# A 256-token hybrid layer on one core: the products of a weight piece in two runs instead of in turn

## The chip, the core and the metric

The kernel runs on one core of one Trainium2 chip. The time is the device time of one execution in microseconds (us). Times of single instructions come from one execution that the hardware profiler recorded. TensorE is called PE in the rows, VectorE DVE, ScalarE ACT, GpSimd POOL, SyncE SP. The start of a matmul is a recorded time; its end is modelled, so that neighbouring matmuls overlap in the rows. What a matmul costs in a stream is therefore read from one start to the next, and not from its duration.

## What is computed

One layer of a bidirectional encoder on 256 tokens of 2048 features, in float32:

```
x = x + 1/2 SwiGLU_1(RMSNorm(x))                  2048 -> 5632 -> 2048
h = RMSNorm(x);  [q|k|v|u|y] = h @ W_in
A = attention(q, k, v);  R = (scan_fwd(conv u) + scan_bwd(conv u)) * gelu(y)
x = x + concat([A, R]) @ W_out
x = x + 1/2 SwiGLU_2(RMSNorm(x))
x = x + sigmoid(RMSNorm(x) @ W_gate) * (p @ W_ple)
out = RMSNorm(x)
```

## The kernel before

**Two parts of 12 bits.** To come near float32 with matmuls that keep fewer bits, every operand is held as a sum of a high and a low part (`split`, line 80: ACT casts the high part, line 81, and DVE subtracts it from the source, line 82). A product of two operands is then high by high, high by low and low by high. The activations lie as `[P, 2, S]`: for 128 features the 256 high parts and beside them the 256 low parts.

**The pair.** `unit_mm` (line 108) makes the three products with two matmuls. The wide one (line 115) has the weights' high part `wh` as stationary operand and streams all 512 columns of the activations into a bank `ps` of PSUM. The small one (line 111) has the weights' low part `wl` as stationary operand and streams the 256 high columns into the second half of the same bank. Each matmul brings its own weight load.

**The unit.** `unit` (line 130) makes 128 output features for all tokens. It walks over the contraction in steps of 128 features, one pair each, all of them added up in one bank. The weights come as one tile per DMA (`weights`, line 119), 16 steps wide (or 11 for `w2`), and are split in pieces of eight steps (8 and 8, or 8 and 3); `spl_pair` gives a piece its two buffers, `whi` and `wlo`, of which there are four each. The FFNs' first layers, the projections to u and y, the output projection and the gate use units of 16 steps. The FFNs' second layers (`w2`, 32 units in each FFN) use units of 22 steps in four pieces (8, 3, 8, 3).

**Other users of PE.** `lead` (line 235) does the first three units together while the first operands arrive. `proj` (line 146) makes q, k and v the other way round: there the activations are stationary and 512 columns of split weights are streamed, three matmuls for each product (`mm3`, lines 89 to 91). The gates of the scans (`scan_job`) use `mm3` with 256 columns. `embed` uses two pairs per call. At the end the last two gate units take their small products in one run (line 633) and their wide ones in halves of 256 columns (line 642).

**Order.** A scheduler lays out each engine's list in advance, from the order in which the code is written, from priorities and from its own simulated times. PE works its list off in order. A piece's first wide matmul waits for ACT's cast, its first small one for DVE's subtraction, and the two buffers come free when PE has done with them.

Of the kernel before, what the change touches and what calls it, by code (L numbers as in the profile page):

```python
# [18 lines left out]
P = 128  # L19
D = 2048  # L20
S = 256
NH = S // P
FF = 5632
C = 512
NKD = D // P
# [3 lines left out]
EPS = 1e-6  # L29
HD = 128  # L30
GRID_W = 64
THETA = 10000.0

# Columns of the packed per-channel parameters.
O_G1, O_GM, O_G2, O_GP, O_GF = 0, 16, 32, 48, 64
# [5 lines left out]
LEAD = (0, 0), (1, 0), (0, 1)  # L41
# [4 lines left out]
def hymba_layer(ctx, tc, xT, pT, w1a, w3a, w2a, win, wqkv, lruw, wout, w1b, w3b, w2b,  # L46
# [31 lines left out]

# [1 line left out]
    def split(src, hi, lo, eng=None):  # L80
# [25 lines left out]

# [1 line left out]
    def unit_mm(ps, wh, wl, a, first, last, cols=slice(0, S)):  # L108
        """a: [P, 2, S], the parts of the activations; the small terms go to the second half."""
        def small():  # L110
            nc.tensor.matmul(ps[:, 1, cols], lhsT=wl, rhs=a[:, 0, cols], start=False, stop=False)  # L111

        if last and not first:
            small()
        nc.tensor.matmul(ps[:, :, cols], lhsT=wh, rhs=a[:, :, cols], start=first, stop=last and not first)  # L115
        if first or not last:
            small()

# [11 lines left out]
    def unit(aT, srcs, nk):  # L130
        """aT: [P, 2, S] per 128 features of the contraction; srcs: DRAM tiles of nk of them."""
        ps = acc.tile([P, 2, S], F32, tag="acc", name="acc")
        at, n = 0, nk * len(srcs)
        for src in srcs:
            for wh, wl in weights(src, nk):
                unit_mm(ps, wh, wl, aT[at], at == 0, at == n - 1)
                at += 1
        tick()
        return ps
# [4 lines left out]

# [1 line left out]
    def proj(aT, srcs):  # L146
# [27 lines left out]

# [1 line left out]
    warm = sml.tile([P, 1], F32, tag="warm", name="warm", bufs=1)  # L176
# [17 lines left out]
    def rsqrt(dst, ssum, n, width):  # L194
        """dst = (ssum / n + EPS) ** -0.5"""
        v = sml.tile([P, 8], F32, tag="rs_v", name="rs_v")[:, :width]
        nc.vector.tensor_scalar(v, ssum, 1.0 / n, EPS, op0=ALU.mult, op1=ALU.add)
        nc.gpsimd.tensor_tensor(dst, v, mhalf[:, :width], op=ALU.pow)

    def inv_rms(*ssq, halves=range(NH), keep=True):  # L200
        """ssq: [P, S], squares summed over blocks of features; all their partitions add up.
        -> 1 / rms per token, as [P tokens, NH] and as [P, S] on every partition."""
        ps = trp.tile([P, 2, S], F32, tag="tr", name="sums")
        n = len(halves)
        for i, h in enumerate(halves):
            for j, s in enumerate(ssq):
                nc.tensor.matmul(ps[:, 0, i:i + 1], lhsT=s[:, h * P:(h + 1) * P], rhs=ones[:, 0:1],
                                 start=j == 0, stop=j == len(ssq) - 1)
        r = sml.tile([P, NH], F32, tag="inv", name="inv", bufs=2)[:, :n]
        rsqrt(r, ps[:, 0, :n], D, n)  # L210
        dg = tmp("dg")
        pb = trp.tile([P, 2, S], F32, tag="tr", name="rows")
        for i in range(n):
            cols = slice(i * P, (i + 1) * P)
            nc.vector.tensor_scalar(dg[:, cols], ident, r[:, i:i + 1], None, op0=ALU.mult)
            nc.tensor.matmul(pb[:, 0, cols], lhsT=ones, rhs=dg[:, cols], start=True, stop=True)
        if not keep:
            return r, pb[:, 0, :n * P]
        rB = sml.tile([P, S], F32, tag="rB", name="rB", bufs=2)
        nc.scalar.copy(rB, pb[:, 0, :])  # L220
        return r, rB

    def add_square(ssq, n, cols=slice(0, S), eng=None):
        """ssq (+)= xs[n] ** 2"""
        if n == 0:
# [9 lines left out]
    def lead():  # L235
        """The first operands in small pieces, in the order of their use; two units at once."""
        aT = act_tiles()
        ps = [acc.tile([P, 2, S], F32, tag="acc", name="acc") for _ in LEAD]
        at = 0
        for n in PIECES:  # L240
# [10 lines left out]
            for m in range(len(LEAD)):  # L251
                split(raw[m][:, js, :], sp[m][0][:, js, :], sp[m][1][:, js, :])
                if m == 0:
                    for k in range(at, at + n):
                        split_gain(xs[:, k, :], par_at(O_G1 + k), aT[k][:, 0, :], aT[k][:, 1, :])
            for k in range(at, at + n):
                for m in range(len(LEAD)):
                    unit_mm(ps[m], sp[m][0][:, k % 8, :], sp[m][1][:, k % 8, :], aT[k], k == 0, k == NKD - 1)
            at += n
# [46 lines left out]

# [1 line left out]
    begun = [None]  # L308
    early = tc.cur_priority + 1000
    am, (rm, rmB) = ffn(*lead(), w1a, w3a, w2a, O_GM)  # L310

# [1 line left out]
    late = tc.cur_priority  # L313
# [11 lines left out]

    # -8 softplus(-lambda), with log1p(e) = 2 atanh(e / (2 + e))
    cneg = const.tile([P, 16], F32, name="cneg")
# [21 lines left out]

# [1 line left out]
    def conv(o, i, blk):  # L351
# [6 lines left out]

# [1 line left out]
    def scan_job(g, u):  # L360
# [65 lines left out]

# [1 line left out]
    def head_rms(src, nh, half):  # L428
        """src: [P tokens, nh HD] -> 1 / rms of each head."""
        ss = sml.tile([P, 4], F32, tag="qss", name="qss")[:, :nh]  # L430
# [7 lines left out]
    def rotate(src, nh, half, m):  # L438
        """[P tokens, nh HD] times the norm's gain, rotated."""
        sv = src.rearrange("p (h d) -> p h d", d=HD)  # L440
# [24 lines left out]
    def transposed(blocks, at, evac):  # L465
        """blocks[h]: [P tokens, .]; two blocks of columns from at on."""
        ps = trp.tile([P, 2, S], F32, tag="tr", name="tr")
# [75 lines left out]

# [1 line left out]
    def y_job(g, y):  # L545
# [24 lines left out]

# [1 line left out]
    ap, (_, rpB) = ffn(a2, inv_rms(ssq2), {}, w1b, w3b, w2b, O_GP)  # L572

# [1 line left out]
    pr = mtile("pr")  # L575
# [9 lines left out]
    def embed(n):  # L585
# [3 lines left out]
        ps = trp.tile([P, 2, S], F32, tag="tr", name="pe")  # L589
        for k in range(2):  # L590
            unit_mm(ps, wh[:, k, :], wl[:, k, :], pp[:, k, :, :], k == 0, k == 1)
        t = tok.tile([P, S], F32, tag="tok", name="pe")
# [22 lines left out]

    # The last features go one half of the tokens after the other; so does the last norm.
    pe = [embed(n) for n in (NKD - 2, NKD - 1)]
# [42 lines left out]
def _units(w, kc=None):  # L660
    """[K, N] -> [N / P, K / (kc P), P, kc P], each tile contiguous."""
    k, n = w.shape
# [5 lines left out]
def _tiles(w):  # L668
    """[K, N] -> [N / C, K / (4 P), P, 4 C], each tile contiguous."""
    k, n = w.shape  # L670
# [4 lines left out]
def _cols(v):  # L675
    """[..., n P] -> [P, ... n]: a channel per partition."""
    return np.ascontiguousarray(v.reshape(-1, P).T)


def _features(v):  # L680
    """[S, n P] -> [P, n S]"""
    return np.ascontiguousarray(v.T.reshape(-1, P, S).transpose(1, 0, 2)).reshape(P, -1)
# [64 lines left out]
```

## Time and profile before

| | |
|---|---|
| median of 3 runs | 1936.04 us (1935.06 to 1936.06) |
| span of the profiled execution, first to last instruction | 1934.1 us |
| PE busy | 98% of the span |
| DVE, ACT, POOL busy | 64%, 51%, 15% |
| share of PE in the chain that ended last | 94% |
| mean granted clock of PE | 0.992 |

The span and the median differ by 1.9 us, which lie outside the first and the last instruction. Shares of busy time are averages over the span; the chain that ended last goes back from the last instruction to what released it, and so on to the start. Nearly all of that chain is matmuls of the two lines 115 and 111, one behind the other.

### The profile page before, as it was taken

Reading aid. Unit: us, or ns where it says so; the run is one execution under the profiler, and the core shown is the slowest. Engines: PE = TensorE matmul, PEld = TensorE weight load, DVE = VectorE, ACT = ScalarE, POOL = GpSimd, SP = SyncE. Lnnn points to the kernel's source line nnn. Section 1 sums busy time; section 2 is a strip of 40 time slices with the busy share of each in tenths; the row PEclk is TensorE's granted clock in tenths of the full one; section 3 lists DMA queues with packets and bytes.
Section 4 is the critical chain, followed back from the end, with each engine's and each line's share of the span. In section 5 each row is a group of like instructions: output and inputs, shape, how many; then the busy total and the mean of one; then the engine's idle time right before and its main releaser. Section 6 shows DMA issues by size and latency. Waiting matters only on the chain.

```text
span 1934.1 us, 26888 instructions
## 1 busy us (share of the span) xinstructions
PE 1895.7 (98%) x10664; PEld 1639.5 (85%) x10664; DVE 1231.6 (64%) x1723; ACT 980.7 (51%) x1490; POOL 286.4 (15%) x231
## 2 busy tenths in 40 slices
PE   7999999999999999998999999999999999999997
PEld 5888888888888888876888888888888888888886
DVE  6766655566666556888777656665556666665686
ACT  4544444444444455586664545454344445545553
POOL 3111100001111000374211111110001111001132
PEclk8999999999999999999999999999999999999998
DMA  6555545565555456534445555554565555555642
GB/s 219 189 193 182 188 163 180 188 211 195 177 193 182 160 192 207 195 137 150 150 152 193 178 188 182 192 174 166 192 213 182 189 186 185 209 188 182 210 161 79
DMA packets 61262, 350.74 MB, mean 181 GB/s; under 512 B 6480, under 2 KB 12112, under 8 KB 31056
## 3 DMA queue, kind: packets, MB, share of 16 engines
q1 hardware_dynamic: 61136, 349.03, 52.9%
q8 instruction: 83, 1.36, 0.3%
q14 instruction: 43, 0.35, 0.1%
HBM read 346.90 MB, written 2.10 MB: 180 GB/s over the span
## 4 chain that ended last, share of the span: by engine, by line
PE 94%; DVE 2%; ACT 2%; DMA 1%; issue 1%; SPq 0%; POOL 0%; POOLq 0%; DVEq 0%; ACTq 0%
PE acc L115 60%; PE acc L111 30%; DVE gate L410 1%; DMA raw<-in_w3a 0%; DVE wlo L82 0%; PE acc L642 0%; PE pe L115 0%; DMA lead<-in_w1a 0%; SPq L101 0%; PE po L508 0%; PE tr L481 0%; PE acc L90 0%; PE acc L91 0%; ACT whi L81 0%; PE acc L89 0%
## 5 line engine op out<-in xcount | busy, mean ns | idle before, releaser
L115 PE MATMUL acc<-aT,whi 128*128 128x512 f32 x3296 | 1156.3, 400 | 10.0 <-DVE aT L86 10.0
L82 DVE TENSOR_TENSOR wlo<-raw,whi 128x1024 fp32r<-128x1024 f32 x722 | 799.9, 1116 | 301.6 <-ACT whi L81 294.9
L81 ACT CAST whi<-raw 128x1024 fp32r<-128x1024 f32 x722 | 689.9, 956 | 482.8 <-PE acc L115 422.0
L111 PE MATMUL acc<-aT,wlo 128*128 128x256 f32 x3296 | 894.6, 282 | 0.0
L115 PEld LDWEIGHTS acc<-aT,whi 128*128 128x128 f32 x3296 | 608.1, 189 | 145.7 <-DVE aT L86 13.1
L111 PEld LDWEIGHTS acc<-aT,wlo 128*128 128x128 f32 x3296 | 624.0, 189 | 20.6
L115 PE MATMUL acc<-hT,whi 128*128 128x512 f32 x1408 | 493.2, 399 | 0.0
L111 PE MATMUL acc<-hT,wlo 128*128 128x256 f32 x1408 | 385.1, 281 | 0.0
L115 PEld LDWEIGHTS acc<-hT,whi 128*128 128x128 f32 x1408 | 260.5, 188 | 59.6
L290 POOL TENSOR_TENSOR s<-s,rB 128x256 f32<-128x256 f32 x88 | 110.5, 1255 | 1103.7 <-ACT s L287 1103.7
L111 PEld LDWEIGHTS acc<-hT,wlo 128*128 128x128 f32 x1408 | 265.8, 189 | 6.4
L301 DVE SCALAR_TENSOR_TENSOR xs<-acc,xs 128x256 f32<-128x256 f32 x128 | 53.8, 420 | 142.7 <-PE acc L115 142.7
L142 ACT COPY z<-acc 128x256 f32<-128x256 f32 x88 | 32.7, 372 | 156.3 <-PE acc L115 156.3
L142 ACT COPY u<-acc 128x256 f32<-128x256 f32 x88 | 32.7, 371 | 154.4 <-PE acc L115 154.4
L230 POOL TENSOR_TENSOR ssq<-ssq,sqr 128x256 f32<-128x256 f32 x58 | 54.2, 934 | 339.8 <-ACT sqr L229 339.8
L115 PE MATMUL acc<-mixT,whi 128*128 128x512 f32 x256 | 89.5, 399 | 1.4 <-DVE mixT L82 1.4
L143 DVE TENSOR_TENSOR u<-acc,u 128x256 f32<-128x256 f32 x88 | 37.2, 423 | 83.2 <-ACT u L142 83.1
L143 DVE TENSOR_TENSOR z<-acc,z 128x256 f32<-128x256 f32 x88 | 37.3, 424 | 83.0 <-ACT z L142 83.0
L111 PE MATMUL acc<-mixT,wlo 128*128 128x256 f32 x256 | 69.3, 281 | 0.0
L115 PEld LDWEIGHTS acc<-mixT,whi 128*128 128x128 f32 x256 | 47.1, 188 | 12.0 <-DVE mixT L82 1.8
L85 ACT ACTIVATE aT<-xs,par_sb 128x256 fp32r<-128x256 f32 x64 | 31.5, 507 | 47.9 <-DVE xs L301 43.9
L86 DVE SCALAR_TENSOR_TENSOR aT<-xs,par_sb,aT 128x256 fp32r<-128x256 f32 x64 | 48.0, 762 | 6.9 <-ACT aT L85 3.4
(169 smaller groups left out, 1051.4 us busy)
## 6 DMA issues: line engine op xcount, KB each, us to landing
raw<-in_w2a SPq DMA_DIRECT2D x64, 704.0 KB, 4.0
raw<-in_w1b SPq DMA_DIRECT2D x44, 1024.0 KB, 5.0
raw<-in_w3b SPq DMA_DIRECT2D x44, 1024.0 KB, 4.9
raw<-in_w2b SPq DMA_DIRECT2D x64, 704.0 KB, 4.0
raw<-in_w3a SPq DMA_DIRECT2D x43, 1024.0 KB, 4.9
raw<-in_w1a SPq DMA_DIRECT2D x42, 1024.0 KB, 4.9
raw<-in_win SPq DMA_DIRECT2D x16, 1024.0 KB, 4.9
raw<-in_wout SPq DMA_DIRECT2D x16, 1024.0 KB, 4.8
```

The costliest lines, as they stand in the source:

```text
L81: nc.scalar.copy(hi, src)
L82: (eng or nc.vector).tensor_tensor(lo, src, f32(hi), op=ALU.subtract)
L85: nc.scalar.activation(hi, src, AF.Copy, scale=gain)
L86: nc.vector.scalar_tensor_tensor(lo, src, gain, f32(hi), op0=ALU.mult, op1=ALU.subtract)
L111: nc.tensor.matmul(ps[:, 1, cols], lhsT=wl, rhs=a[:, 0, cols], start=False, stop=False)
L115: nc.tensor.matmul(ps[:, :, cols], lhsT=wh, rhs=a[:, :, cols], start=first, stop=last and not first)
L142: nc.scalar.copy(t, ps[:, 1, cols])
L143: nc.vector.tensor_tensor(t, ps[:, 0, cols], t, op=ALU.add)
L230: (eng or nc.gpsimd).tensor_tensor(ssq[:, cols], ssq[:, cols], t, op=ALU.add)
L290: nc.gpsimd.tensor_tensor(s, s, rB, op=ALU.mult)
L301: nc.vector.scalar_tensor_tensor(xs[:, n, :], ps[:, j, :], 0.5, xs[:, n, :], op0=ALU.mult, op1=ALU.add)
L410: nc.vector.tensor_tensor_scan(i[d][:, k, rev], a[d][:, k, rev], r[d][:, k, rev], 0.0, op0=ALU.mult, op1=ALU.add)
```

## The change

`unit_mm` is gone. `unit_mms` takes the weights of a whole piece and issues all its wide matmuls first and then all its small ones. The number of matmuls, their operands and shapes, the DMAs and the splits are the same. A bank is now opened by the piece's first wide matmul and closed by its last small one. `unit`, `lead` and `embed` call it with pieces of 8 (or 3), of 1 to 4, and of 2 steps.

```diff
-    def unit_mm(ps, wh, wl, a, first, last, cols=slice(0, S)):
-        """a: [P, 2, S], the parts of the activations; the small terms go to the second half."""
-        def small():
-            nc.tensor.matmul(ps[:, 1, cols], lhsT=wl, rhs=a[:, 0, cols], start=False, stop=False)
-
-        if last and not first:
-            small()
-        nc.tensor.matmul(ps[:, :, cols], lhsT=wh, rhs=a[:, :, cols], start=first, stop=last and not first)
-        if first or not last:
-            small()
+    def unit_mms(ps, ws, acts, first, last):
+        n = len(ws)
+        for i in range(n):
+            nc.tensor.matmul(ps, lhsT=ws[i][0], rhs=acts[i], start=first and i == 0, stop=False)
+        for i in range(n):
+            nc.tensor.matmul(ps[:, 1, :], lhsT=ws[i][1], rhs=acts[i][:, 0, :], start=False,
+                             stop=last and i == n - 1)
...
         for src in srcs:
-            for wh, wl in weights(src, nk):
-                unit_mm(ps, wh, wl, aT[at], at == 0, at == n - 1)
-                at += 1
+            ws = weights(src, nk)
+            for j in range(0, nk, 8):
+                part = ws[j:j + 8]
+                unit_mms(ps, part, aT[at:at + len(part)], at == 0, at + len(part) == n)
+                at += len(part)
...
-            for k in range(at, at + n):
-                for m in range(len(LEAD)):
-                    unit_mm(ps[m], sp[m][0][:, k % 8, :], sp[m][1][:, k % 8, :], aT[k], k == 0, k == NKD - 1)
+            for m in range(len(LEAD)):
+                unit_mms(ps[m], [(sp[m][0][:, k % 8, :], sp[m][1][:, k % 8, :]) for k in range(at, at + n)],
+                         aT[at:at + n], at == 0, at + n == NKD)
...
-        for k in range(2):
-            unit_mm(ps, wh[:, k, :], wl[:, k, :], pp[:, k, :, :], k == 0, k == 1)
+        unit_mms(ps, [(wh[:, k, :], wl[:, k, :]) for k in range(2)], [pp[:, k, :, :] for k in range(2)],
+                 True, True)
```

In the lists below `whi` marks a wide matmul (line 115 before, line 113 in the changed kernel) and `wlo` a small one (line 111 before, line 115 in the changed kernel). A number behind a name is that of the buffer; each `aT` buffer holds four steps of the contraction and each `hT` buffer two.

PE's list before, in the first layer of FFN 1, from the end of one unit (bank `acc_1826`) to the start of the next (`acc_1869`):

```order
L111 MATMUL acc_1826<-aT_110,wlo_1834 128x256
L115 MATMUL acc_1826<-aT_110,whi_1833 128x512
L111 MATMUL acc_1826<-aT_110,wlo_1834 128x256 x2
L115 MATMUL acc_1826<-aT_110,whi_1833 128x512
L115 MATMUL acc_1869<-aT_107,whi_1872 128x512
L111 MATMUL acc_1869<-aT_107,wlo_1873 128x256
```

The same unit in the changed kernel:

```order
L113 MATMUL acc_1826<-aT_107,whi_1829 128x512 x4
L113 MATMUL acc_1826<-aT_108,whi_1829 128x512 x4
L115 MATMUL acc_1826<-aT_107,wlo_1830 128x256 x4
L115 MATMUL acc_1826<-aT_108,wlo_1830 128x256 x4
L113 MATMUL acc_1826<-aT_109,whi_1833 128x512 x4
L113 MATMUL acc_1826<-aT_110,whi_1833 128x512 x4
L115 MATMUL acc_1826<-aT_109,wlo_1834 128x256 x4
L115 MATMUL acc_1826<-aT_110,wlo_1834 128x256 x4
L113 MATMUL acc_1869<-aT_107,whi_1872 128x512 x4
```

Where the two kinds took turns, with two in a row only at the unit's end, eight wide ones now stand in a row and then eight small ones.

PE's list in the changed kernel at the start of the second layer of FFN 1, the first half of a unit of 22 steps:

```order
L113 MATMUL acc_2420<-hT_360,whi_2423 128x512 x2
L113 MATMUL acc_2420<-hT_361,whi_2423 128x512 x2
L113 MATMUL acc_2420<-hT_362,whi_2423 128x512 x2
L113 MATMUL acc_2420<-hT_363,whi_2423 128x512 x2
L115 MATMUL acc_2420<-hT_360,wlo_2424 128x256 x2
L115 MATMUL acc_2420<-hT_361,wlo_2424 128x256 x2
L115 MATMUL acc_2420<-hT_362,wlo_2424 128x256 x2
L115 MATMUL acc_2420<-hT_363,wlo_2424 128x256 x2
L113 MATMUL acc_2420<-hT_364,whi_2427 128x512 x2
L113 MATMUL acc_2420<-hT_365,whi_2427 128x512
L115 MATMUL acc_2420<-hT_364,wlo_2428 128x256 x2
L115 MATMUL acc_2420<-hT_365,wlo_2428 128x256
```

Here runs of eight and runs of three follow each other.

PE's list in the changed kernel at the start of the mixing stage, where the last step's activations (the fourth step of `aT_5684`) come latest (`sums` adds up the squares for the norm):

```order
L113 MATMUL acc_6896<-aT_5683,whi_6903 128x512 x4
L113 MATMUL acc_6896<-aT_5684,whi_6903 128x512 x3
L113 MATMUL acc_6947<-aT_5681,whi_6950 128x512 x4
L113 MATMUL acc_6947<-aT_5682,whi_6950 128x512 x4
L115 MATMUL acc_6947<-aT_5681,wlo_6951 128x256 x4
L115 MATMUL acc_6947<-aT_5682,wlo_6951 128x256 x4
L113 MATMUL acc_6947<-aT_5683,whi_6954 128x512 x4
L208 MATMUL sums_6836<-ones_103,ssq_5685 128x1 x2
L113 MATMUL acc_6896<-aT_5684,whi_6903 128x512
L115 MATMUL acc_6896<-aT_5683,wlo_6904 128x256 x4
L115 MATMUL acc_6896<-aT_5684,wlo_6904 128x256 x4
```

The scheduler has put twenty matmuls of the second unit (`acc_6947`) between the first unit's 15th and its 16th wide one.

## Rows read from the trace of the kernel before

**Rows 1.** The page: busy time per engine, granted clock in 40 slices, chain by engine

```profile
PE 1895.7 (98%) x10664; PEld 1639.5 (85%) x10664; DVE 1231.6 (64%) x1723; ACT 980.7 (51%) x1490; POOL 286.4 (15%) x231
...
PEclk8999999999999999999999999999999999999998
...
PE 94%; DVE 2%; ACT 2%; DMA 1%; issue 1%; SPq 0%; POOL 0%; POOLq 0%; DVEq 0%; ACTq 0%
```

**Rows 2.** Groups: line, engine, operation, out<-in, shape, count | busy, mean ns | idle before

```profile
L115 PE MATMUL acc<-aT,whi 128*128 128x512 f32 x3296 | 1156.3, 400 | 10.0 <-DVE aT L86 10.0
...
L115 PE MATMUL acc<-hT,whi 128*128 128x512 f32 x1408 | 493.2, 399 | 0.0
...
L115 PE MATMUL acc<-mixT,whi 128*128 128x512 f32 x256 | 89.5, 399 | 1.4 <-DVE mixT L82 1.4
```

**Rows 3.** Timeline of PE at a unit's end: start, length (modelled), line, operation, count

```profile
600.22 0.40 PE L111 MATMUL acc<-aT,wlo 128*128 128x256 f32 x2
600.46 0.63 PE L115 MATMUL acc<-aT,whi 128*128 128x512 f32 x2
600.93 0.28 PE L111 MATMUL acc<-aT,wlo 128*128 128x256 f32 x1
601.05 0.40 PE L115 MATMUL acc<-aT,whi 128*128 128x512 f32 x1
```

**Rows 4.** Chain that ended last, in time: start, time in the chain, what

```profile
334.92 0.47 PE acc L115 x2
342.69 0.47 PE acc L115 x2
...
549.75 0.47 PE acc L115 x2
...
594.97 0.47 PE acc L115 x2
```

**Rows 5.** Timeline of PE in the mixing stage: scan gates (tr) and a projection

```profile
824.63 0.28 PE L89 MATMUL tr<-uc_hi,gw_hi 128*128 128x256 f32 x1
...
824.98 0.28 PE L89 MATMUL tr<-uc_hi,gw_hi 128*128 128x256 f32 x1
...
825.58 0.28 PE L91 MATMUL tr<-uc_hi,gw_lo 128*128 128x256 f32 x1
...
826.06 0.40 PE L89 MATMUL acc<-whi,aT 128*128 128x512 f32 x1
826.30 0.40 PE L90 MATMUL acc<-wlo,aT 128*128 128x512 f32 x1
826.53 0.39 PE L91 MATMUL acc<-whi,aT 128*128 128x512 f32 x1
826.76 0.40 PE L89 MATMUL acc<-whi,aT 128*128 128x512 f32 x1
...
827.23 0.39 PE L91 MATMUL acc<-whi,aT 128*128 128x512 f32 x1
...
827.90 0.39 PE L91 MATMUL acc<-whi,aT 128*128 128x512 f32 x1
...
831.53 0.28 PE L89 MATMUL tr<-uc_hi,gw_hi 128*128 128x256 f32 x1
```

**Rows 6.** Timeline of PE near the end: 24 small matmuls of line 633 in a row

```profile
1907.08 3.04 PE L633 MATMUL small<-aT,wlo 128*128 128x256 f32 x24
1909.96 0.52 PE L642 MATMUL acc<-aT,whi 128*128 128x256 f32 x3
```

**Rows 7.** Waits of PE: engine, line, waited for, us in total, times, longest

```profile
PE acc L90 <- DVE wlo L82: 11.3, 4, 4.7
PE acc L115 <- DVE aT L86: 10.0, 8, 3.2
```

**Rows 8.** Busy time by stretch, the mixing stage's middle, with the clock behind POOL

```profile
830.00:912.00 82.00, 69.47 (x313) 56.37 (x312) 66.05 (x61) 58.29 (x94) 51.00 (x22) 0.94 0.41 141
```

**Rows 9.** Groups: ACT's casts of weight pieces, with the idle time before them

```profile
L81 ACT CAST whi<-raw 128x1024 fp32r<-128x1024 f32 x722 | 689.9, 956 | 482.8 <-PE acc L115 422.0 <-PE acc L91 17.2 <-issue 15.6
```

## The prediction

> **What bounds the kernel now.** First the page [rows 1]: PE is busy 98% of the span, holds 94% of the chain that ended last, and its granted clock stands at nine tenths or more in 38 of 40 slices. PE's list is the path; DVE (64%) and ACT (51%) are beside it nearly everywhere. So the question is not who waits, but how closely PE can start one matmul after another, and whether that depends on their order.
>
> Second, the groups [rows 2]: 3296 + 1408 + 256 wide matmuls are 206 x 16, 64 x 22 and 16 x 16 steps. From the code, the 206 hold the lead's three units, so 219 units of 16 steps are outside it; each has two pieces of eight, 438. The 64 units of `w2` have two pieces of eight and two of three. Together that is **566 pieces of eight and 128 pieces of three**; what else uses pairs (the lead's 48, the embedding's 32) is a sixtieth of the whole.
>
> Third, the price of a piece now. In the chain [rows 4] the pair of wide matmuls that closes one unit and opens the next stands at 549.75 and again, eight units later, at 594.97: 45.22 us for 16 pieces of eight, **2.826 us a piece**, 0.3533 a pair. For `w2` it stands at 334.92 and 342.69: 7.77 us for 22 pairs, again 0.353, so a piece of three costs 1.060. At full clock these streams have no gaps: what a pair costs is PE's own pace.
>
> Fourth, what runs cost. Outside the lead the trace has no run of more than two wide matmuls from `unit_mm`, but the mixing stage has the changed kernel's pattern with other operands [rows 5]: 12 small ones of a scan's gates (256 columns) and then a long run of 512-column ones of a projection, each with a weight load of its own.
> - Small ones after wide ones: from 824.63 to 826.06 twelve in 1.43 us; the first eight, up to 825.58, in **0.95 us**. The first three take 0.35 us (to 824.98).
> - Wide ones after small ones: the first eight, from 826.06 to 827.90, in **1.84 us**. They don't start at their final pace: the first three take 0.70 us (to 826.76), while from 827.23 to 831.53 there are 19 in 4.30 us, 0.2263 each. The switch costs some 0.03 us, spread over the first five.
> - Small ones of exactly this kind in a long run [rows 6]: 24 in 2.88 us, 0.120 each, the gates' pace.
>
> So a pair costs 0.353 us in alternation, and 0.2263 + 0.120 = 0.346 us if its halves stand in long runs. Alternation pays for a switch at every pair.
>
> **The change part by part.**
> *A piece of eight* becomes one run of eight wide and one of eight small: 1.84 + 0.95 = 2.79 us instead of 2.826, a gain of 0.036. One row stands for 2.79 and is rounded to a hundredth, so 0.036 is good to about 0.01. 566 x 0.036 = **20.4 us**, and 15 to 26 with the rounding.
> *A piece of three*: 0.70 + 0.35 = 1.05 instead of 1.060; 128 x 0.010 = **1.3 us** (0 to 2.5).
> *Unit ends*: the old order put two small and two wide side by side there; this is inside the 2.826. In the new order a unit begins and ends as any piece does.
> *Buffers and waits*: nothing is added. A piece's first wide one follows the piece before it as it did, so ACT's cast is due when it was; the first small one comes 1.84 us later in its piece, where it came one wide matmul (0.235) later, so DVE's part is due later. The `whi` buffer comes free one run of small ones earlier (0.95 us); ACT, which is idle 422 us waiting for PE to free such buffers [rows 9], casts that much earlier into a queue that PE reaches in the same order. Taken at nothing; this hides behind the three other buffers, and without them a late cast would delay a whole run.
> *Stage starts*: the last step's activations are now due in the middle of the second piece, after 2.79 + 7 x 0.23 = 4.4 us, where it was 15 x 0.353 = 5.3 us. The list fills this: twenty matmuls of the second unit stand before the first unit's last wide one. At nothing; if that cover failed, 0.9 us at each of three stages.
> *Lead and embedding*: the lead's matmuls wait for activations, 10.0 us in eight waits [rows 7], and these arrive as before. The embedding's four matmuls have as many switches as before. Taken at nothing, with +-1.5 us.
> *Mixing stage*: between 830 and 912 us PE is busy only 69.5 of 82 us, at a granted clock of 0.94 on average [rows 8]; its longest wait is 4.7 us for a split on DVE [rows 7]. Chains of ACT, DVE and POOL set the end there. ACT's and DVE's lists are a little rearranged near it. I put it at nothing, and +-5 us, one such wait, into the range.
>
> Sum: 20.4 + 1.3 = 21.7 us. I round it to 21, since the 16 units of u and y that lie beside the waiting chains may not pass on all of theirs. The span of 1934.1 becomes 1913; with the 1.9 us by which the median of the runs exceeds it, **1915 us**, 1.1% less.
>
> **The rivals.**
> *R1, wide matmuls of a unit don't get faster in a run* (slower). At each unit's end two of them stand in a row, from 600.46 to 600.93 [rows 3]: 0.235 each, as slow as in alternation. If that is their pace in any run, because they stream activations where the projection streams weights, a piece costs 8 x (0.235 + 0.120) = 2.84 us, 0.014 more, and a piece of three 1.065: 566 x 0.014 + 128 x 0.005 = 9 us, **1945 us**. It decides from a mean of (2.826 - 0.95) / 8 = 0.2345 us per wide one in a run. For it: all that the trace shows of these operands in a row. Against it: the projection's first two after small ones cost 0.24 and 0.23 as well [rows 5], so two in a row can't tell; and the small ones cost 0.120 with either kind of operand.
> *R2, order doesn't matter*: what a pair costs is tied to its two matmuls, and 0.353 against 0.346 comes from the operands. Then 1936 us, within 4.
> By the Trainium skill, page "TensorE: Matmul & The Clock Gate", section "Back-to-back issue gap", a warm matmul follows the one before after its columns divided by 2.4 GHz plus 2.5 ns. By that rule a pair would cost an estimated 325 ns in any order, and R2 would be the result. The rows don't follow it: both runs and the alternation are slower, and by different amounts, which is why R2 gets little.
> *R3, no slow start*: if the first five wide ones of a run come at the final pace too, a piece costs 8 x 0.2263 + 0.95 = 2.76 us; 566 x 0.066 + 128 x 0.031 = 41 us, **1895 us**. Against it: every start of a projection after small ones shows the slow first steps.
> *R4, the runs aren't there*: the scheduler could have broken them up. The new list shows runs of eight nearly everywhere, so this has no chance of its own.
>
> **How the numbers follow.** The forecast gets 0.70, R1 0.11, R2 0.11, R3 0.08. The forecast's own range is 1915 +6 and -5 for the rounding, and +-5 for the mixing stage, not added in full: 1907 to 1923. Widened toward R3 below and R2 above until about 2 in 10 are left out: **1905 to 1927**. Within 0.2% (3.9 us) is about what a measurement of this kernel can't tell from no change. Faster by more: 0.70 + 0.08 and a little of R2's neighbourhood, 0.79; same 0.10; slower 0.11.
>
> **What would show it.** In the timeline of a unit: a piece's eighth wide matmul to its first small one and back, 1.84 and 0.95 us; the first wide ones 0.23 to 0.24 apart and the last three 0.227; small ones 0.120 apart. Units of 16 steps 5.58 us apart instead of 5.65, units of 22 steps 7.68 instead of 7.77. PE's waits in total as before, within 5 us. It is wrong if the eighth wide one still stands 0.235 after the seventh (R1), if the unit still takes 5.65 (R2), or if units are faster and the end is not, with new waits in the mixing stage.

## The result, and the profile after

The changed kernel takes **1923.58 us** (median of 4 runs, 1922.13 to 1924.14) where the kernel before takes 1935.91 (4 runs beside it, 1935.06 to 1936.06): a ratio of 0.9936, 95% interval 0.9921 to 0.9950. That is 12.3 us or 0.64% less, inside the range of 1905 to 1927, and 8.6 us above the forecast of 1915. The profiled execution spans 1921.8 us instead of 1934.1. The reason given for the gain turned out to be wrong, as the last experiment shows.

The page of the changed kernel, the lines that answer to [rows 1] and, of the groups (columns as in [rows 2]), those that answer to [rows 2] and [rows 9]. Line 113 is now the wide matmul and line 115 the small one:

```profile
PE 1879.3 (98%) x10664; PEld 1645.7 (86%) x10664; DVE 1214.0 (63%) x1723; ACT 964.6 (50%) x1490; POOL 304.6 (16%) x231
...
PEclk8999999999999999999999999999999999999998
...
PE 92%; DVE 3%; ACT 2%; DMA 1%; issue 1%; POOL 1%; SPq 0%; POOLq 0%; DVEq 0%; ACTq 0%
...
L81 ACT CAST whi<-raw 128x1024 fp32r<-128x1024 f32 x722 | 689.5, 955 | 833.1 <-PE acc L113 572.3
L113 PE MATMUL acc<-aT,whi 128*128 128x512 f32 x3296 | 835.4, 394 | 9.7 <-DVE aT L86 9.6
```

PE is the path as before, and ACT waits for PE to free the buffers even longer than in [rows 9], so the casts are nowhere late in the FFNs. The pieces can be read directly. The timeline of PE in the first layer of FFN 1 (start, modelled length, line, operation, count):

```profile
600.53 1.11 PE L115 MATMUL acc<-aT,wlo 128*128 128x256 f32 x8
601.48 2.00 PE L113 MATMUL acc<-aT,whi 128*128 128x512 f32 x8
603.33 1.11 PE L115 MATMUL acc<-aT,wlo 128*128 128x256 f32 x8
604.28 2.00 PE L113 MATMUL acc<-aT,whi 128*128 128x512 f32 x8
606.12 0.64 PE L115 MATMUL acc<-aT,wlo 128*128 128x256 f32 x4
```

(The last line is cut off by the end of the stretch asked for.) From start to start, eight wide ones take 1.85 and 1.84 us and eight small ones 0.95: a piece is 2.80 and 2.79 us long, as forecast. PE's waits, against [rows 7] (us in total, times, longest):

```profile
PE acc L90 <- DVE wlo L82: 12.7, 5, 4.7
PE acc L113 <- DVE aT L86: 9.6, 6, 2.9
...
PE tr L500 <- DVE pt L493: 2.3, 2, 1.8
PE acc L113 <- DVE mixT L82: 1.4, 1, 1.4
...
PE po L509 <- ACT pT_sb L502: 1.0, 1, 1.0
```

The wait for `pt` is new. `pt` holds a block of attention's probabilities on its way to being turned (`tr`, line 500) and multiplied with v (`po`, line 509). The stretch of [rows 8], with PE's granted clock behind POOL:

```profile
830.00:912.00 82.00, 67.94 (x307) 54.65 (x307) 67.35 (x64) 59.55 (x104) 47.56 (x21) 0.94 0.40 139
```

PE is busy 1.5 us less of the 82 than before, but the same clock times hold other work here: in the changed kernel the projections to q, k and v begin 7.5 us earlier. From that stage's first product to the next stage's, PE is busy 80.75 of 94.81 us (811.70 to 906.51) where it was 80.65 of 93.18 (819.16 to 912.34), so what was added there is idle time.

Since the kernel runs through stages one after the other, the starts of the stages' first products in the traces say where the time went. All numbers are us. "Mixing grouped" and "no turn" are the experiments `h1_mix_only` and `i1_no_flip` below; a second profile of the same kernel stands in brackets. Each column is one profiled execution. The profiles of `e1_out2_alt`, `g_ffn_only` and `f2_run16_out2`, quoted further down, are of the fastest of their four executions, 2.4 to 2.9 us under the median.

| from the first product of one stage to that of the next | before | after | mixing grouped | no turn |
|---|---|---|---|---|
| start, lead, 41 units | 272.8 (273.8) | 272.1 (269.5) | 269.3 | 267.9 |
| first quarter of `w2`, 16 units of 22 steps; the same four times | 124.37 | 122.68 | 122.03 | 122.03 |
| 44 units of 16 steps; again in FFN 2 | 248.75 | 245.80 | 244.05 | 244.05 |
| u, 8 units, with the norm | 48.86 | 48.44 | 48.45 | 48.28 |
| projections to q, k, v | 93.2 (92.0) | 94.8 (95.3) | 94.8 | 94.5 |
| y, 8 units, attention | 61.3 | 61.0 | 61.0 | 61.2 |
| out-projection, 16 units, with attention's last block | 95.2 (95.2) | **99.3 (99.4)** | 99.3 | 94.5 |
| first 44 units of FFN 2, with the norm | 249.6 | 246.7 | 245.1 | 245.0 |
| gate and end | 118.2 | 117.1 | 117.6 | 116.9 |

The FFNs gave what was forecast: 2.95 us on 44 units, 1.69 on each quarter of `w2`, four times. Two stages lost: the out-projection 4.1 us, the projections 1.6.

**What happened at the out-projection.** In the order of the contraction, attention's last block gives steps 6 and 7. The list starts with the six steps ahead of them, of two units (12 pairs), while DVE and ACT still make the last block. PE's timeline of the kernel before, with the idle time and its releaser in brackets:

```profile
975.73 0.38 PE L499 MATMUL tr<-ident,pt 128*128 128x128 f32 x2
975.86 0.48 PE L115 MATMUL acc<-mixT,whi 128*128 128x512 f32 x1
976.17 0.28 PE L111 MATMUL acc<-mixT,wlo 128*128 128x256 f32 x1
...
978.03 0.82 PE L499 MATMUL tr<-ident,pt 128*128 128x128 f32 x6
979.25 1.99 PE L508 MATMUL po<-pT_sb,v_sb 128*128 128x256 f32 x8 [0.40 <-ACT pT_sb L501]
982.65 0.50 PE L115 MATMUL acc<-mixT,whi 128*128 128x512 f32 x1 [1.40 <-DVE mixT L82]
```

And of the changed kernel:

```profile
967.51 2.91 PE L113 MATMUL acc<-mixT,whi 128*128 128x512 f32 x12
972.24 0.56 PE L500 MATMUL tr<-ident,pt 128*128 128x128 f32 x2 [1.82 <-DVE pt L493]
973.24 0.87 PE L500 MATMUL tr<-ident,pt 128*128 128x128 f32 x6 [0.44 <-DVE pt L493]
975.07 3.58 PE L509 MATMUL po<-pT_sb,v_sb 128*128 128x256 f32 x8 [0.95 <-ACT pT_sb L502]
980.05 0.73 PE L113 MATMUL acc<-mixT,whi 128*128 128x512 f32 x2 [1.40 <-DVE mixT L82]
```

Before, pairs stood between the transposes and covered them. Now the piece that holds the last block's two steps can issue six wide ones, but its small ones stand behind the two wide ones that have to wait. Two units give 12 wide matmuls of cover and no small ones, and PE waits 1.82 + 0.44 + 0.95 us where it waited 0.40. Then the `po` matmuls take 3.58 us instead of 1.99. The busy times by stretch (columns as in [rows 8]) say why:

```profile
968.00:975.30 7.30, 4.08 (x20) 2.81 (x19) 5.33 (x14) 7.23 (x16) 0.72 (x1) 1.00 0.42 144
975.30:978.70 3.40, 3.35 (x8) 2.10 (x7) 0.00 (x0) 0.22 (x2) 0.00 (x0) 0.50 0.00 0
```

After a stretch in which PE was busy 4.1 of 7.3 us, the granted clock is 0.50 (1.2 GHz instead of 2.4) for 3.4 us. The kernel before has 1.00 there.

### The profile page after: what moved, and what is told of

The parts are those of the page before. It is cut to its first block, busy times and chain, and to the rows that moved or that the text cites. A ratio compares the mean times of both kernels' runs of the same rounds, so it can differ in the third digit from the quotient of the medians.

```text
span 1921.8 us, 27287 instructions
## 1 busy us (share of the span) xinstructions
PE 1879.3 (98%) x10664; PEld 1645.7 (86%) x10664; DVE 1214.0 (63%) x1723; ACT 964.6 (50%) x1490; POOL 304.6 (16%) x231
## 4 chain that ended last, share of the span: by engine, by line
PE 92%; DVE 3%; ACT 2%; DMA 1%; issue 1%; POOL 1%; SPq 0%; POOLq 0%; DVEq 0%; ACTq 0%
PE acc L113 59%; PE acc L115 30%; DVE wlo L82 1%; DVE gate L411 1%; ACT whi L81 0%; PE po L509 0%; DMA raw<-in_w3a 0%; PE acc L643 0%; PE pe L113 0%; SPq L101 0%; DMA lead<-in_w1a 0%; PE tr L482 0%; DMA raw<-in_wqkv 0%; DVE uc L357 0%; PE sums L208 0%
## 5 line engine op out<-in xcount | busy, mean ns | idle before, releaser
L113 PE MATMUL acc<-aT,whi 128*128 128x512 f32 x3296 | 835.4, 394 | 9.7 <-DVE aT L86 9.6
L115 PEld LDWEIGHTS acc<-aT,wlo 128*128 128x128 f32 x3296 | 452.7, 191 | 32.6
L115 PE MATMUL acc<-aT,wlo 128*128 128x256 f32 x3296 | 464.4, 283 | 0.0
L113 PE MATMUL acc<-hT,whi 128*128 128x512 f32 x1408 | 364.8, 392 | 0.0
L115 PEld LDWEIGHTS acc<-hT,wlo 128*128 128x128 f32 x1408 | 202.7, 190 | 21.3
L115 PE MATMUL acc<-hT,wlo 128*128 128x256 f32 x1408 | 209.0, 282 | 0.0
L90 PE MATMUL acc<-wlo,aT 128*128 128x512 f32 x96 | 39.9, 415 | 12.7 <-DVE wlo L82 12.7
L293 DVE TENSOR_TENSOR u<-u,s 128x256 f32<-128x256 f32 x88 | 37.4, 425 | 9.2 <-DVE u L144 0.5
L82 DVE TENSOR_TENSOR hT<-u,hT 128x256 fp32r<-128x256 f32 x88 | 38.0, 432 | 1.9 <-ACT hT L81 1.9
L287 DVE TENSOR_TENSOR z<-z,rB 128x256 f32<-128x256 f32 x88 | 37.4, 425 | 2.8
```

The costliest lines, as they stand in the source:

```text
L82: (eng or nc.vector).tensor_tensor(lo, src, f32(hi), op=ALU.subtract)
L90: nc.tensor.matmul(ps, lhsT=ah, rhs=wl, start=False, stop=False)
L113: nc.tensor.matmul(ps, lhsT=ws[i][0], rhs=acts[i], start=first and i == 0, stop=False)
L115: nc.tensor.matmul(ps[:, 1, :], lhsT=ws[i][1], rhs=acts[i][:, 0, :], start=False, stop=last and i == n - 1)
L287: nc.vector.tensor_tensor(z, z, rB, op=ALU.mult)
L293: nc.vector.tensor_tensor(u, u, s, op=ALU.mult)
```

## The experiments

Kernels of one group ran on one chip, beside runs of the kernel before. The theory at the outset was the prediction's: alternation pays for a switch at each pair, the runs save it, and the rest was lost at the out-projection (A) or elsewhere (B). Line numbers in these kernels differ by one or two.

### The out-projection's first two units in turn, and the lead in turn

`e1_out2_alt` gives `unit` a length of run, which is eight everywhere but in the two units that cover attention's last block:

```diff
-    def unit(aT, srcs, nk):
+    def unit(aT, srcs, nk, run=RUN):
...
-            for j in range(0, nk, 8):
-                part = ws[j:j + 8]
+            for j in range(0, nk, run):
+                part = ws[j:j + run]
...
-        ps = unit(mixT, [wout[n, 0]], NKD)
+        ps = unit(mixT, [wout[n, 0]], NKD, 1 if n < 2 else RUN)
```

> The changed kernel, but the first two units of the output projection take turns again (runs of one), as before; all else stays in runs of eight. Theory A (lost cover): in the changed kernel those two units could only give 12 wide matmuls while the last attention block was under way, since the small ones of a piece stand behind all its wide ones, and two of those wait for that block; PE then waited 4.2 us more around 970 to 980 us and ran at the lower clock for 3.4 us. With turns the 12 small ones come back as cover: about 1.9 us of waits go (to 0.4 + 1.4 us as before), the lower clock there goes, and the time is about 5 us less than the changed kernel's 1923.6, 1918 to 1920. Theory B (the loss comes from the rearranged lists of ACT and DVE): the waits stay and the time is 1923 to 1925.

Measured: 1921.9 us (1919.48 to 1922.66), ratio 0.9928 (0.9911 to 0.9944). The stage falls from 99.3 to 96.3 us, the waits for `pt` from 2.3 to 0.8, and the stretch of lower clock is gone. Three of the five us lost there (4.1 us more where 1.1 less was counted) come back in the profile, 1.7 in the median, which lies between the ranges of A and B; the intervals of this ratio and of the changed kernel's overlap, so it is the stage's trace that speaks for A.

`e2_lead_alt` keeps the runs of eight and puts the lead back in turn:

```diff
-            for m in range(len(LEAD)):
-                unit_mms(ps[m], [(sp[m][0][:, k % 8, :], sp[m][1][:, k % 8, :]) for k in range(at, at + n)],
-                         aT[at:at + n], at == 0, at + n == NKD)
+            for k in range(at, at + n):
+                for m in range(len(LEAD)):
+                    unit_mms(ps[m], [(sp[m][0][:, k % 8, :], sp[m][1][:, k % 8, :])],
+                             aT[k:k + 1], k == 0, k == NKD - 1)
```

> The changed kernel, but the lead's three units take turns step by step as before; all else stays in runs of eight. Theory A (the lead lost 2.2 us): in the changed kernel the first layer of FFN 1 ended only 0.6 us earlier, where its 41 later units alone save 2.8; small matmuls that filled waits for activations now stand behind wide ones that wait. With turns the lead is as before and the time about 2 us less than 1923.6, 1921 to 1922.5. Theory B (the loss is a matter of where the lower clock falls in the first 50 us, and not of the order): within 1 us of 1923.6.

Measured: 1923.5 us (1922.93 to 1924.26), ratio 0.9935 (0.9920 to 0.9950). The first stage is 271.7 us long, against 272.1 and 269.5 in two profiles of the changed kernel. The order in the lead makes no difference that can be seen.

### Longer and shorter runs

With `unit` as in `e1_out2_alt`, `RUN = 16` and `RUN = 4` for all units (a tile of `w2` has 11 steps):

> The changed kernel with runs as long as a weight tile: 16 wide, then 16 small in units of 16 steps, 11 and 11 in those of w2. Theory A (each cycle of a wide and a small run costs a fixed 0.019 us over the two final paces 0.2267 and 0.120): units of 16 steps go from 5.58 to 5.56 us, those of w2 by 0.02 less, 219 x 0.019 + 64 x 0.02 = 5 us less in the units; the attention's cover gets no better, so 1918 to 1920 if nothing else waits. Theory B (the cost is in proportion to the matmuls, not to the switches): units stay at 5.58 and the time at 1923.6. A third outcome is that PE waits for weight pieces, of which two are now held to the end of a unit: then new waits on L81 or L82 stand in the trace and the time is over 1925.

> The changed kernel with runs of four (4 wide, 4 small; 4, 4 and 3 in w2). Theory A (the slow start is spread over the first five wide ones of a run): four wide ones cost 0.234 + 0.236 + 0.228 + 0.232 = 0.93 us and four small ones 0.472, so units of 16 steps take 4 x 1.402 = 5.61 us and those of w2 7.71: 219 x 0.028 + 64 x 0.02 = 7.5 us more in the units than with runs of eight; some of the attention's cover comes back (first small ones stand behind four wide ones instead of eight), 0 to 4 us: 1927 to 1931. Theory B (only the first wide matmul after a small one is dear): units at 5.57 to 5.59 and the time 1920 to 1924.

Measured: 1919.83 us (1918.98 to 1921.14) for 16, ratio 0.9916 (0.9901 to 0.9931), and 1928.21 (1927.1 to 1929.81) for 4, ratio 0.9959 (0.9945 to 0.9974). The 44 units take 244.93 and 246.97 us, so a unit of 16 steps takes 5.567 with runs of 16, 5.586 with 8 and 5.613 with 4: one more wide run and small run costs 0.019 us from 16 to 8 and 0.014 from 8 to 4, much as theory A had it. In `w2` it doesn't hold: runs of 11 gain nothing over 8 and 3 (122.67 against 122.68 us), and with runs of 4, 4 and 3 a unit takes 7.68 us (122.90 for sixteen), not 7.71. The out-projection stays at 99.0 and 98.9 us in both.

### Runs in the FFNs only, and a better place for the late block

`g_ffn_only` has runs of eight in the FFNs and the gate; the lead is as in `e2_lead_alt`, and the three calls of `unit` in the mixing stage get run 1:

```diff
-            ps = unit(am, [win[4 * g + k, 0]], NKD)
+            ps = unit(am, [win[4 * g + k, 0]], NKD, 1)
...
-            ps = unit(am, [win[8 + 4 * g + k, 0]], NKD)
+            ps = unit(am, [win[8 + 4 * g + k, 0]], NKD, 1)
...
-        ps = unit(mixT, [wout[n, 0]], NKD)
+        ps = unit(mixT, [wout[n, 0]], NKD, 1)
```

> Runs of eight only in the two FFNs and the gate; the lead and all units of the mixing stage (u, y, output projection) take turns as before. Theory A (the pieces gain what was forecast, and the losses come from the mixing stage and the lead, where the order took cover away): the FFN halves are as short as in the changed kernel, 2.9 us less for 44 units of 16 and 1.7 us less for 16 units of 22, 18.3 us in all with the first 41 units, and 1.1 us in the gate; the rest as before, so 19.4 us less than before, 1916 to 1918.5, better than the changed kernel although 32 units fewer are in runs. Theory B (the mixing stage or the first 50 us lose time in any kernel whose FFN is faster): 1920 to 1924.

Measured: 1919.41 us (1916.54 to 1920.61), ratio 0.9914 (0.9899 to 0.9929). Thirty-two units fewer in runs, and yet 4 us better than the changed kernel: the out-projection takes 94.6 us, as A expected, though the median lies between the ranges of A and B. The stage is also 0.7 us shorter than in the kernel before, although in both the pairs are taken in turn, which the theory at the outset doesn't explain. This was the first sign that it was not the turns that cost.

`f2_run16_out2` joins `RUN = 16` with the two units in turn of `e1_out2_alt`. `f1_run16_parts` instead lets the two units issue their products in four runs, with steps 8 to 11 ahead of the late steps 6 and 7:

```diff
+            if parts:
+                for p in parts:
+                    unit_mms(ps, [ws[k] for k in p], [aT[k] for k in p], p is parts[0], p is parts[-1])
+                continue
...
-        ps = unit(mixT, [wout[n, 0]], NKD)
+        ps = unit(mixT, [wout[n, 0]], NKD, RUN, (range(6), range(8, 12), range(6, 8), range(12, 16)) if n < 2 else None)
```

> Runs of 16 (11 in w2), but the first two units of the output projection take turns. If the lost cover at the last attention block is worth what the run with turns in those two units showed (3 us in the stage's own trace), this is 2 to 3 us less than runs of 16 alone (1919.8): 1916.5 to 1918. If it isn't, 1919 to 1921.

> Runs of 16 (11 in w2), but the first two units of the output projection walk over the contraction in another order and in shorter pieces: six steps whose activations are there, four of the scan's first half, the two of the last attention block, four of the scan's second half. Theory A (cover): 20 pairs instead of 12 wide matmuls, some 7 us instead of 2.8, are ahead of the wait for the last attention block; all waits around 970 to 980 us (4.2 us more than before in the changed kernel, and before's own 1.8) go or nearly go, and the lower clock there too: 5 to 6 us less than runs of 16 alone, 1913.5 to 1916. Theory B (the scan's outputs come too late to cover): waits for mixT from another source stand there instead and the time is 1918 to 1921.

Measured: 1917.55 us (1914.68 to 1918.47), ratio 0.9904 (0.9889 to 0.9919), stage 96.0; and 1913.97 (1913.73 to 1914.69), ratio 0.9889 (0.9872 to 0.9905), stage 94.0. With the ready steps 8 to 11 moved ahead of the late ones the stage loses nothing against the kernel before (95.2). With the two units only in turn it still loses 0.8 us, as it lost 1.1 in `e1_out2_alt`, and waits for `pt` (0.6 us) and `pT_sb` (0.9) remain.

In the same group the kernel before was profiled again:

> The kernel before once more, for a second profile of its first 60 us. In every profile with runs of four and more PE is at the lower clock for 3.4 us shortly after the 24 one-column matmuls of the lead's norm (at 41 to 47 us); in the first profile of before it isn't. If that comes from the order, it is absent here too; if it is a matter of chance where these matmuls fall, it may stand here as well, and the first layer of FFN 1 then ends some 1.7 us later than 272.6.

Measured: 1935.72 us, span 1933.9. The first stage is 1.0 us longer than in the first profile and the projections 1.2 us shorter, so differences of that size in these two stages are not the order's. FFNs and out-projection agree to the hundredth. The 3.4 us at the lower clock do stand in this profile (41.5 to 44.9 us), and they are missing in the second profile of the changed kernel below: they come and go without a change of order.

### The mixing stage alone, and the late block with runs of eight

`h1_mix_only` is `g_ffn_only` the other way round: `RUN = 1`, so the FFNs and the gate are in turn, as is the lead, and the three calls in the mixing stage get run 8. `h2_run8_parts` is `f1_run16_parts` with `RUN = 8`. The changed kernel ran once more beside them.

> Runs of eight in the 32 mixing units alone (the 8 u units, the 8 y units, the 16 of the out-projection); the lead, both FFNs and the gate alternate as in the kernel before. Theory A (in the mixing stage the grouping costs more than it gives, because the last attention block loses the cover of twelve small products): the stage from the first out-projection product to the first one of the second FFN grows from 95.2 to 98 to 99.5 us, with the wait for pt back at about 2 us; u and y units give back 0.3 to 0.5 us each; the whole is slower than the kernel before by 2 to 4 us, ratio 1.001 to 1.002. Theory B (the stage suffers only because TensorE reaches it earlier, out of faster FFN units): out-projection at 94 to 95 us, the whole faster by 1 to 2.5 us.

> The changed kernel (runs of eight) with one difference: the first two out-projection units issue their products in runs over weight tiles 0-5, 8-11, 6-7, 12-15, so that all that does not need the last attention block stands ahead of the two tiles that do. Theory A: the wait for pt goes (from 2.3 us), the one for pT_sb falls to 0.4, no stretch of the lower granted clock at the out-projection, the stage falls from 99.3 to 94 to 95 us, the whole to 1917.5 to 1920 us. Rival (the loss sits elsewhere, and the shorter stage is given back later): 1921.5 to 1924.

> The changed kernel once more, unaltered, beside the two others on the same chip: 1922 to 1925 us. Theory A: the waits of the last attention block stand as in the first profile (pt 2.3, pT_sb 1.0, mixT 1.4 us), so the loss there belongs to the order. The stretch of lower clock after the 24 one-column sums near 41 us and the lower clock at the out-projection are read again: what comes and goes between two profiles of one kernel is not the order's.

Measured: `after_again` 1923.36 us (1921.85 to 1924.96), ratio 0.9939 (0.9925 to 0.9953), with the three waits of the last block to the tenth as before (2.3, 1.4 and 1.0); its first stage is 2.6 us shorter than in the first profile, its out-projection 99.4. `h2_run8_parts` 1917.75 (1916.71 to 1918.59), ratio 0.9907 (0.9894 to 0.9920): 5.6 us better than the changed kernel by a change to two units, and the stage takes 94.3 us. Its timeline:

```profile
966.66 2.45 PE L114 MATMUL acc<-mixT,whi 128*128 128x512 f32 x10
968.95 0.88 PE L116 MATMUL acc<-mixT,wlo 128*128 128x256 f32 x6
...
973.63 1.03 PE L505 MATMUL tr<-ident,pt 128*128 128x128 f32 x8
975.06 1.99 PE L514 MATMUL po<-pT_sb,v_sb 128*128 128x256 f32 x8 [0.40 <-ACT pT_sb L507]
```

The wait for `pt` is gone, the one for `pT_sb` is 0.40, and `po` takes 1.99 us again. The loss at the out-projection is shown to be the cover.

`h1_mix_only` was to be slower than the kernel before (A) or faster by 1 to 2.5 us (B). Neither came: it takes **1914.12 us** (five of six runs from 1912.46 to 1914.91, one at 1928.69), ratio 0.9899 (0.9877 to 0.9921). The out-projection lost its 4.1 us as expected (99.3). But the FFNs, in turn, are faster than with any runs: 244.05 us for 44 units, 5.547 a unit. So the theory at the outset is wrong: taking wide and small ones in turn costs nothing by itself. What differs from the kernel before in the FFNs is only the last step of a unit. There `unit_mm` issued the small one first, so that two small ones and then, with the next unit, two wide ones stood side by side [rows 3]; `unit` with run 1 never turns round.

### No turn at a unit's end

`i1_no_flip` is the kernel before with this one difference; nothing is grouped.

```diff
     def unit_mm(ps, wh, wl, a, first, last, cols=slice(0, S)):
...
-        def small():
-            nc.tensor.matmul(ps[:, 1, cols], lhsT=wl, rhs=a[:, 0, cols], start=False, stop=False)
-
-        if last and not first:
-            small()
-        nc.tensor.matmul(ps[:, :, cols], lhsT=wh, rhs=a[:, :, cols], start=first, stop=last and not first)
-        if first or not last:
-            small()
+        nc.tensor.matmul(ps[:, :, cols], lhsT=wh, rhs=a[:, :, cols], start=first, stop=False)
+        nc.tensor.matmul(ps[:, 1, cols], lhsT=wl, rhs=a[:, 0, cols], start=False, stop=last)
```

> The kernel before with one difference: its pair is always wide, then small; it no longer turns round at the last step of a unit (before: small ahead of wide there, so that two small and then two wide ones stood side by side at each unit's end). Nothing is grouped. Theory C (formed from the run with the mixing stage alone grouped, where the FFNs alternated without that turn and a pair cost 0.3467 us, no more than in long runs; alternation costs nothing by itself, the turn at each unit's end throws the stream into a slower cadence of 0.3533): units of 16 steps 5.55 us apart and of 22 steps 7.63 apart in both FFNs, 23 us less for 219 units of 16 and 9 us less for 64 units of 22, some 2 to 4 us given back at the projections: 1904 to 1909 us. If the second FFN starts in the slower cadence it keeps it: then 1918 to 1924. Theory A (alternation pays for a switch at every pair, as the prediction said): 5.65 and 7.77 us, 1934 to 1937.

Measured: **1907.50 us** (1906.32 to 1907.85), ratio **0.9855** (0.9838 to 0.9871): the best of all, more than twice the gain of the change under study, by an edit of one helper. The profile spans 1904.4 us. PE's timeline in the first layer of FFN 1, a stretch with a unit's end in it that can no longer be told from the rest:

```profile
600.02 0.39 PE L110 MATMUL acc<-aT,whi 128*128 128x512 f32 x1
600.25 0.28 PE L111 MATMUL acc<-aT,wlo 128*128 128x256 f32 x1
600.37 0.39 PE L110 MATMUL acc<-aT,whi 128*128 128x512 f32 x1
...
605.57 0.39 PE L110 MATMUL acc<-aT,whi 128*128 128x512 f32 x1
```

Sixteen pairs in 5.55 us, 0.347 each. This is just what a wide and a small one cost in the inside of long runs, 0.2263 + 0.120 [rows 5, 6]. The table's last column has the rest: 4.70 us on 44 units, 2.34 on each quarter of `w2`, and no loss at the out-projection. Theory C stands for the FFNs. The edit also moves `stop`, which closes the bank, from the unit's last wide matmul to its last small one. That flag doesn't set the pace: with `stop` on the small one `g_ffn_only` has stretches at the slow pace, and with it on the wide one the kernel before has units at the fast one (both shown below).

## Why the prediction was right, and where it was wrong

**The terms of the sum.** "A piece of eight" (2.79 instead of 2.826) and "a piece of three" (1.05 instead of 1.060) came out to the hundredth: 5.586 us for a unit of 16 steps, forecast 5.58; 7.667 for one of 22, forecast 7.68. They were read from rows that showed both patterns. R1 and R3 fell with that, and R2 with it: order does matter, by up to 0.0067 us a pair.

**The step that was mis-sized** is "Mixing stage ... at nothing", with "Stage starts ... if that cover failed, 0.9 us at each of three". The forecast was 21.7 us in the span, rounded to 21, and 12.3 came. With 1923.58 us the time lies just above the forecast's own range of 1907 to 1923 and only within the one widened toward the rivals. The out-projection took 4.1 us more where 1.1 less was counted (16 units at 0.07): 5.2 us, shown by `e1_out2_alt`, `g_ffn_only`, `f1_run16_parts` and `h2_run8_parts` to be the lost cover. The prediction asked at stage starts only when the last step's activations are due, and not what else stands behind them: in a run, the small products of ready steps stand behind wide ones that wait. The place stood in [rows 2], where `mixT` has a wait of 1.4 us ahead of its products, and was not followed to the list there. The rest, some 4 us, lies in the first stage and the projections. In the first stage two profiles of one kernel differ by 1.0 and 2.6 us, so nothing is to be explained there; the means of the two profiles of each kernel, 273.3 and 270.8, are 2.5 us apart, near the 2.95 that 41 units were to give. The projections take 94.2 to 95.3 us in every kernel with faster FFNs, whatever the order in the mixing stage, against 93.2 and 92.0 before: PE comes earlier to a chain of splits on ACT and DVE that keeps its own pace (longest wait 4.7 us in both). That this is the cause is argued from the rows and was not tried, and as the two profiles of the kernel before differ by 1.2 us here, part of it may be chance.

**The step that was wrong** is the reading behind the sum: "Alternation pays for a switch at every pair." It rested on the mean of whole units and on two kinds of long runs, and put the whole difference of 0.353 to 0.346 down to the turns. The trace of before had the counter-example, in the second unit after the lead, and it was not looked for. Its timeline, from that unit to the next:

```profile
47.12 0.39 PE L115 MATMUL acc<-aT,whi 128*128 128x512 f32 x1
...
51.63 0.39 PE L115 MATMUL acc<-aT,whi 128*128 128x512 f32 x1
51.86 0.40 PE L111 MATMUL acc<-aT,wlo 128*128 128x256 f32 x2
52.10 0.63 PE L115 MATMUL acc<-aT,whi 128*128 128x512 f32 x2
...
52.67 0.40 PE L115 MATMUL acc<-aT,whi 128*128 128x512 f32 x1
...
57.26 0.40 PE L115 MATMUL acc<-aT,whi 128*128 128x512 f32 x1
57.50 0.40 PE L111 MATMUL acc<-aT,wlo 128*128 128x256 f32 x2
```

From 47.12 to 51.63 thirteen pairs take 4.51 us, 0.347 each; then comes the turn at the unit's end, and from 52.67 to 57.26 thirteen pairs take 4.59 us, 0.353 each, and so in every later unit of the FFNs. The same order of the same matmuls, at the same granted clock, has two paces. So the change gained 0.0042 us a pair by breaking up the slow cadence, and would have gained 0.0067 by leaving the pairs in turn and taking away only the turn round at the unit's end. That the forecast's units were right in spite of this is because the runs were priced from rows of runs, and not from a theory of the turns.

## What to carry to other kernels

Before a stream is regrouped, look through the whole trace for places where the same order already runs faster, and for what stands right ahead of the slow stretch: a mean over units hides both. When accumulating matmuls are grouped, ask at each place where PE waits for late data which ready matmuls now stand behind the late ones; order those units by readiness, as `h2_run8_parts` does for 5.6 us. A forecast whose size is right can still have the wrong cause, and only an experiment that removes the supposed cause alone tells.

## What the runs showed of the hardware

Wide and small matmuls in strict turn run at one of two paces, and hold it. In `i1_no_flip` one stretch of 2068 pairs, from 46.05 us in FFN 1 into the units to u, and one of 2100 pairs, from 1066.46 us in FFN 2 into the gate, hold 0.3467 us a pair. In `g_ffn_only`, in the units to u, the timeline shows the other, also in strict turn:

```profile
774.20 0.39 PE L114 MATMUL acc<-aT,whi 128*128 128x512 f32 x1
...
800.69 0.40 PE L114 MATMUL acc<-aT,whi 128*128 128x512 f32 x1
```

75 pairs in 26.49 us, 0.3532 each. From start to start the faster one repeats 0.230 and 0.117 us in `i1_no_flip`; the slower one repeats every three pairs (0.241, 0.120, 0.236, 0.113, 0.232, 0.118), which adds 0.02 us to three pairs. A pace changes only where the turn is broken: by two of one kind, other matmuls or a wait. After the bare turn at a unit's end (two small ones, then two wide ones, nothing between) it is the slow one in all units of the FFNs. It needn't be: in the out-projection of the kernel before, in both of its profiles, one unit goes on at the fast pace right behind such a turn. In the first profile:

```profile
989.31 0.40 PE L111 MATMUL acc<-mixT,wlo 128*128 128x256 f32 x2
989.54 0.63 PE L115 MATMUL acc<-mixT,whi 128*128 128x512 f32 x2
...
990.13 0.39 PE L115 MATMUL acc<-mixT,whi 128*128 128x512 f32 x1
...
994.64 0.39 PE L115 MATMUL acc<-mixT,whi 128*128 128x512 f32 x1
```

Thirteen pairs in 4.51 us, 0.347 each, and the slow pace behind the next turn. So the turn alone doesn't decide the pace. Which break leads to which pace, and why there are two, stays open: in the second unit after the lead, shown above, the fast pace followed two small ones, four matmuls of line 216 and two wide ones, and in `h1_mix_only` the last eleven gate units in turn, each behind the same break (a pair, then four matmuls of the embedding), take the two paces alternately.

By the gap that the Trainium skill, page "TensorE: Matmul & The Clock Gate", section "Back-to-back issue gap", gives for an isolated matmul, the pair would take an estimated 325 ns; the fastest that the FFNs held in any order here is 346.7.

Against the fast pace, a wide run and a small run cost 0.02 us or less: 0.020 for one of each (runs of 16, 5.567 against 5.547 us a unit), 0.039 for two (runs of 8) and 0.066 for four (runs of 4). In the changed kernel's runs of eight it is spread over the first five wide ones, which on average start 0.234, 0.235, 0.228, 0.231 and 0.230 us apart, against 0.227 for the last three.

And a few us of waiting can cost more than themselves. In the six profiles that lack the cover or part of it (the changed kernel twice, `e2_lead_alt`, `e3_run16`, `e4_run4`, `h1_mix_only`) a stretch of 3.4 to 6.8 us at 1.2 GHz followed and `po` took 1.1 to 1.7 us longer than 1.99; in the other eight there is none. The length of the waits doesn't tell the two apart: for `pt` and `pT_sb` together `e4_run4` waited 1.8 us and fell to 1.2 GHz, `e1_out2_alt` waited 1.8 us too and didn't.
